# The low part of each dense weight tile: an accumulating DMA in place of a subtraction on VectorE

## The chip, the cores and the metric

The kernel runs on one core of one Trainium2 chip. The metric is the device time of one execution, in microseconds (us). Before the change the median of 3 runs is 2462.2 us (2461.52 to 2467.54).

## The reference

Two layers of a diffusion backbone on 512 latent tokens and 256 context tokens, 768 in all, with 1024 features. In each layer an adaLN-modulated RMSNorm feeds three token mixers (windowed attention, a bidirectional HGRN2 recurrence and a gated MLP over chunks) from one input projection; each branch is projected, gated and summed, and an output projection and a SwiGLU FFN follow, both with gated residuals. Context tokens are dropped from layer 1's queries onward, so that most of layer 1 works on 512 tokens.

```python
def merge(a, b, c, gate, w_br, w_o):
    g = jax.nn.sigmoid(gate.reshape(gate.shape[:-1] + (N_BRANCH, D_MODEL)))
    m = g[..., 0, :] * (a @ w_br[0]) + g[..., 1, :] * (b @ w_br[1]) + g[..., 2, :] * (c @ w_br[2])
    return m @ w_o

def swiglu(h, w_gate, w_up, w_down):
    return (jax.nn.silu(h @ w_gate) * (h @ w_up)) @ w_down
...
        y, yc = hybrid_mixer(h, hc, w_in[l], ...)
        x = x + g1 * y
        h = rmsnorm(x, norm2_g[l]) * (1.0 + sc2) + sh2
        x = x + g2 * swiglu(h, w_ffn_gate[l], w_ffn_up[l], w_ffn_down[l])
```

Everything is float32.

## The kernel before

Activations lie with the feature on the partition and the token along the row. Every large product goes through `dense`: it makes 128 output features for a range of tokens, from one weight tile of 128 input rows x `kt` groups (the k-rows) x 128 columns. TensorE multiplies in float32r, which keeps fewer bits than float32. So the weights and the activations are each split in a high part (the value rounded to float32r) and a low part (the rest), and each product is the sum of three: high x high, high weight x low activation, low weight x high activation. In `mms` these come in this order for each k-row, each in pieces of at most 512 columns. A tile with 8 k-rows is thus 24 products, each of 512, 768 (512 + 256) or 256 columns, and the first that needs the low weights is the third.

`load_w` makes a weight tile's parts. SyncE's queue loads `wr` from DRAM (`load_raw`, 3 buffers, shared with the tiles `wra` of the adaLN weights). ACT writes the high part `wh` by a copy (line 286, 2 buffers); VectorE writes the low part `wl` = `wr` - `wh` (line 287, 2 buffers). `load_w` is called 364 times, once for each dense product. Since `wh` and `wl` have two buffers, a tile's parts can be written once the product two before it is done with its buffers, that is, while the product just before it runs.

The products that the prediction speaks of, by stage, in each of the two layers:

- w_in: 34 tiles of 8 k-rows (heads of HGRN, keys, values, queries, the MLP's projections), among which the chains of HGRN and attention are woven in (`step_chain`).
- gate and branch: 24 pairs. The gate tile has 8 k-rows (from `w_in`), the branch tile 4 (from `w_branch`). ACT takes the tanh of the gate's result (line 1126), VectorE multiplies, and POOL adds to `macc` (line 1138).
- w_out: 8 tiles of 8 k-rows for each of two token blocks: 512 and 256 columns in layer 0, 256 and 256 in layer 1.
- FFN: 22 pairs of a gate and an up tile of 8 k-rows, with a silu of the gate's result between (line 1176), in four pieces (`FF_PIECES`, 5, 5, 6, 6). After each piece come 8 tiles of w_ffn_down with 5 or 6 k-rows; the last piece's are made for each of the two token blocks apart (512 and 256 columns, then 256 and 256).

Layer 0 has 768 tokens in all these; layer 1 has 512 from the queries on.

The order on each engine is set by the recording framework's scheduler, from the order in which the program is written and its own estimates of time; each engine, and each DMA queue, then runs its list in order. GpSimd's (POOL's) list holds tensor instructions, such as the sums of squares `sqa`, the rope products and the `macc` sums, and 16 DMAs that put the residual `X` into DRAM and bring it back (lines 588 and 594).

Of the kernel before, what the change touches and what calls it, by code (L numbers as in the profile page):

```python
# [9 lines left out]
F32 = mybir.dt.float32  # L10
# [6 lines left out]
P = 128  # L17
# [33 lines left out]
class Page:  # L51
    """A page of the static arena: one token row block ([P, T]) or two ([P, 2, T])."""
# [8 lines left out]
class Pages:  # L61
    """On-chip pages handed out in program order; the one that is free first by the estimate goes first."""
# [41 lines left out]
class Builder:  # L104
# [45 lines left out]
    def preload(self, func, after):  # L150
        """Has the activation table of func loaded as soon as after is there, before the data for it comes."""
        t = self.small("pre", 1)
        self.nc.scalar.activation(out=t, in_=after, func=func)

    # ---------------------------------------------------------------- setup
# [25 lines left out]
    def columns(self, name, items, queue):  # L181
        """Parameter vectors as columns of one tile, feature on the partition; yields between load and use."""
# [30 lines left out]
    def pcol(self, name, l=0, per=1):  # L213
        """Columns of a parameter: all of them, or those of layer l of per layers."""
        tile, r0, n = self.col[name]
        n //= per
        return self.par[tile][:, r0 + l * n:r0 + (l + 1) * n]
# [56 lines left out]
    # ------------------------------------------------------------- weights  # L274
# [5 lines left out]
    def load_w(self, wap, kt):  # L280
# [6 lines left out]
        nc.vector.tensor_tensor(out=o, in0=r, in1=h.bitcast(F32), op=ALU.subtract)  # L287
# [28 lines left out]
    def spent(self, us):  # L316
        """Advances the estimate of TensorE's clock and gives waiting chains their turns."""
# [20 lines left out]
    # --------------------------------------------------------------- adaLN  # L338
    def ada_fold(self, acc, part):
        """Partial products [128, 512] -> [128, 16]: sums over each 32 partitions, feature % 32 on the partition."""  # L340
# [6 lines left out]
    def ada_spread(self, l, units, parts, nb):  # L347
        """Sums the four partition groups of the parts of some units, each feature on its partition, and adds the bias."""
# [22 lines left out]
    def ada_units(self, l, units, nb):  # L371
        """Steps that make four feature tiles of the modulation for each unit while other work goes on."""
# [22 lines left out]
    def ada_first(self):  # L395
        """Scale and shift of the first norm, which everything waits for; yields within its work."""
# [23 lines left out]
    def ada_rows(self, u, w):  # L420
        """Four feature tiles of layer 0 on TensorE: two rows, turned into columns."""
# [31 lines left out]
    # --------------------------------------------------------------- norms  # L453
    def rstd(self, sq, chunks, inv_n):
        """1/sqrt(mean+eps) per token, a column for each chunk."""
# [15 lines left out]
    def spread(self, rs, chunks):  # L471
        """Spreads a column for each chunk over all partitions: one bank per 512 tokens."""
# [13 lines left out]
    def norm_sums(self, blk):  # L486
        """Squares of the residual's tokens of one block, summed over the feature tiles."""
# [12 lines left out]
    def settle(self, blk, apply, pace, spread=True):  # L500
        """A chain that norms one token block of the residual; apply takes the bank of rstd, by token % 512."""
# [22 lines left out]
    def norm_part(self, blk, rb, k0=0, k1=KD, pool=False):  # L524
        """h = rmsnorm(X)*(1+sc)+sh for one token block, split in float32r parts."""
# [37 lines left out]
    def split_pairs(self, srcs, t1, name):  # L563
        """srcs: float32 pairs, given back here -> act list of (hi, lo), pages held"""
# [14 lines left out]
    # ------------------------------------------------------------ residual  # L579
# [4 lines left out]
    def x_out(self, t1):  # L584
        """The residual isn't used inside a mixer: it waits in DRAM."""
# [41 lines left out]
    # ---------------------------------------------------------------- HGRN  # L627
# [152 lines left out]
    # ----------------------------------------------------------- attention  # L780
# [42 lines left out]
    def attn_queries(self, l, i, act, wcol, tq, ag):  # L823
        """Queries of two heads, each as a column stack of its high and low parts; their blocks join the chains."""
# [503 lines left out]
```

## Time and profile before

| | |
|---|---|
| median of 3 runs | 2462.2 us |
| the profiled execution's span | 2460.2 us |
| TensorE busy | 2410.8 us (98%) |
| VectorE busy | 1426.7 us (58%) |
| ScalarE (ACT) busy | 837.1 us (34%) |
| GpSimd (POOL) busy | 202.6 us (8%) |
| DMA engines, queue q1 (loads from DRAM) | 30.5% of 16 engines' span |
| mean granted TensorE clock | 0.998 |

The profiled execution took 2460.2 us from its first to its last instruction; the median of the runs stands 2.0 us over that. A row of the timeline gives the start in us from the span's start, the duration in us, the engine, the line, and what is written from what; in brackets stands how long the engine was idle before it and what ended that. A row of a group gives the count, the busy time in us, the mean duration in ns, and the idle time before. A row of waits gives the sum in us, the times, and the longest. A row of stretches gives the length and then the busy time and count of PE, PEld (TensorE's weight loads), DVE, ACT and POOL, the granted TensorE clock, the DMA share and GB/s. A row of DMA issues ends with the size in KB and the median us from issue to landing.

### The profile page before, as it was taken

Reading aid. Unit: us, or ns where it says so; the run is one execution under the profiler, and the core shown is the slowest. Engines: PE = TensorE matmul, PEld = TensorE weight load, DVE = VectorE, ACT = ScalarE, POOL = GpSimd, SP = SyncE. Lnnn points to the kernel's source line nnn. Section 1 sums busy time; section 2 is a strip of 40 time slices with the busy share of each in tenths; the row PEclk is TensorE's granted clock in tenths of the full one; section 3 lists DMA queues with packets and bytes.
Section 4 is the critical chain, followed back from the end, with each engine's and each line's share of the span. In section 5 each row is a group of like instructions: output and inputs, shape, how many; then the busy total and the mean of one; then the engine's idle time right before and its main releaser. Section 6 shows DMA issues by size and latency. Waiting matters only on the chain. (4 is left out here: it accounts for less than half of the span.)

```text
span 2460.2 us, 34161 instructions
## 1 busy us (share of the span) xinstructions
PE 2410.8 (98%) x13814; PEld 2074.5 (84%) x13814; DVE 1426.7 (58%) x2452; ACT 837.1 (34%) x1372; POOL 202.6 (8%) x143
## 2 busy tenths in 40 slices
PE   8999999999999999999999999999999999999998
PEld 3888888888888888888888888888888889888888
DVE  4688777875454374745353376668884337434335
ACT  3333344442222342221222253324453335322224
POOL 0000100000111210000000040101000122000001
PEclk9999999999999999999999999999999999999999
DMA  8222111123433243434344351112113335233334
GB/s 293 71 78 78 52 42 37 31 60 108 146 112 90 82 127 97 136 98 144 94 122 118 90 150 58 39 42 60 50 51 107 107 102 160 80 102 101 94 101 131
DMA packets 361869, 236.33 MB, mean 96 GB/s; under 512 B 8112, under 2 KB 333168, under 8 KB 361712
## 3 DMA queue, kind: packets, MB, share of 16 engines
q1 hardware_dynamic: 357776, 221.57, 30.5%
q0 software_dynamic: 2304, 10.49, 1.3%
q8 instruction: 109, 1.79, 0.3%
q10 hardware_dynamic: 1632, 2.10, 0.3%
q14 instruction: 48, 0.39, 0.0%
HBM read 226.78 MB, written 7.34 MB: 95 GB/s over the span
## 5 line engine op out<-in xcount | busy, mean ns | idle before, releaser
L286 ACT ACTIVATE wh<-wr 128x1024 fp32r<-128x1024 f32 (+2 forms) x364 | 344.7, 947 | 1042.7 <-PE pd L304 962.1
L287 DVE TENSOR_TENSOR wl<-wr,wh 128x1024 fp32r<-128x1024 f32 (+2 forms) x364 | 396.3, 1089 | 255.4 <-ACT wh L286 251.8
L304 PE MATMUL pd<-hh,wh 128*128 128x512 f32 (+1 forms) x1504 | 456.6, 359 | 1.0 <-DVE X L624 0.8
L304 PE MATMUL pd<-hh,wl 128*128 128x512 f32 (+1 forms) x1504 | 446.5, 353 | 0.3 <-DVE wl L287 0.3
L304 PE MATMUL pd<-hl,wh 128*128 128x512 f32 (+1 forms) x1504 | 443.9, 351 | 0.0
L304 PE MATMUL pd<-fl,wh 128*128 128x512 f32 (+1 forms) x1072 | 322.3, 352 | 0.0
L304 PE MATMUL pd<-fh,wl 128*128 128x512 f32 (+1 forms) x1072 | 321.8, 351 | 0.3 <-DVE wl L287 0.3
L304 PE MATMUL pd<-fh,wh 128*128 128x512 f32 (+1 forms) x1072 | 321.1, 351 | 0.6 <-ACT silu L1176 0.6
L304 PEld LDWEIGHTS pd<-hh,wl 128*128 128x128 f32 x1504 | 246.7, 188 | 37.6 <-DVE wl L287 0.8
L304 PEld LDWEIGHTS pd<-hl,wh 128*128 128x128 f32 x1504 | 246.5, 189 | 34.0
L304 PEld LDWEIGHTS pd<-hh,wh 128*128 128x128 f32 x1504 | 247.4, 189 | 31.3 <-ACT wh L286 1.2
L368 DVE SCALAR_TENSOR_TENSOR acc<-wra,sc,acc 128x512 f32<-128x512 f32 x224 | 162.1, 755 | 190.5 <-DMA wra<-in_w_ada 140.8
L304 PEld LDWEIGHTS pd<-fh,wl 128*128 128x128 f32 x1072 | 177.6, 188 | 30.0 <-DVE wl L287 1.2
L304 PEld LDWEIGHTS pd<-fh,wh 128*128 128x128 f32 x1072 | 176.9, 188 | 29.3 <-ACT silu L1176 0.8
L304 PEld LDWEIGHTS pd<-fl,wh 128*128 128x128 f32 x1072 | 177.4, 188 | 28.0
L304 PE MATMUL pd<-guh,wl 128*128 128x512 f32 (+1 forms) x576 | 174.8, 340 | 1.1 <-DVE wl L287 1.1
L304 PE MATMUL pd<-guh,wh 128*128 128x512 f32 (+1 forms) x576 | 175.0, 340 | 0.0
L304 PE MATMUL pd<-gul,wh 128*128 128x512 f32 (+1 forms) x576 | 174.5, 339 | 0.0
L1178 DVE TENSOR_TENSOR silu<-pd,silu 128x768 f32<-128x768 f32 (+1 forms) x44 | 36.2, 824 | 164.8 <-PE pd L304 164.8
L624 DVE SCALAR_TENSOR_TENSOR X<-pd,mod,X 128x256 f32<-128x256 f32 (+1 forms) x128 | 65.9, 546 | 94.7 <-PE pd L304 94.6
L304 PEld LDWEIGHTS pd<-guh,wl 128*128 128x128 f32 x576 | 99.5, 189 | 14.2 <-DVE wl L287 1.8
L304 PEld LDWEIGHTS pd<-gul,wh 128*128 128x128 f32 x576 | 99.5, 189 | 12.5
(224 smaller groups left out, 3362.0 us busy)
## 6 DMA issues: line engine op xcount, KB each, us to landing
wr<-in_w_in SPq DMA_DIRECT2D x116, 512.0 KB, 3.8
wra<-in_w_ada SPq DMA_DIRECT2D x80, 512.0 KB, 3.7
wr<-in_w_ffn_gate SPq DMA_DIRECT2D x44, 512.0 KB, 3.8
wr<-in_w_ffn_up SPq DMA_DIRECT2D x44, 512.0 KB, 3.9
wr<-in_w_ffn_down SPq DMA_DIRECT2D x48, 384.0 KB, 3.4
wr<-in_w_out SPq DMA_DIRECT2D x32, 512.0 KB, 4.1
wr<-in_w_branch SPq DMA_DIRECT2D x48, 256.0 KB, 2.8
wr<-in_w_ffn_down SPq DMA_DIRECT2D x32, 320.0 KB, 3.1
```

The source lines that it names most:

```text
L286: nc.scalar.activation(out=h, in_=r, func=AF.Copy)
L287: nc.vector.tensor_tensor(out=o, in0=r, in1=h.bitcast(F32), op=ALU.subtract)
L304: nc.tensor.matmul(ps[:, b0:b1], lhsT=w[:, k, :], rhs=x[:, b0:b1], start=b not in first, stop=(k == kt - 1 and i == 2), skip_group_check=True)
L368: nc.vector.scalar_tensor_tensor(out=acc[:, 0:512], in0=w, scalar=sc, in1=acc[:, 0:512], op0=ALU.mult, op1=ALU.add)
L624: self.nc.vector.scalar_tensor_tensor(out=self.X[m][:, c0:c1], in0=ps[:, c0:c1], scalar=gcol(b, m), in1=self.X[m][:, c0:c1], op0=ALU.mult, ...
L1178: nc.vector.tensor_tensor(out=s[:, 0:tt], in0=pu[:, 0:tt], in1=s[:, 0:tt], op=ALU.mult)
```

## The change

In `load_w` the subtraction on VectorE is gone. ACT, after the high copy, writes the negated raw tile into `wl`, rounded to float32r like the high part, so that `wl` holds minus the high part. Then GpSimd issues a DMA from `wr` to `wl`, both in SBUF, with `accum_op=ALU.add`: the DMA adds `wr` to what stands in `wl`, which leaves the low part. The DMA is issued once ACT's second copy is done, and the products with the low weights wait for its landing. `wr` is held until then too.

```diff
@@ -284,7 +284,8 @@
         lo = self.wl.tile([P, KD, P], F32R, tag="wl", name=self.nm("wl"))
         r, h, o = (t.rearrange("p k c -> p (k c)")[:, 0:kt * P] for t in (raw, hi, lo))
         nc.scalar.activation(out=h, in_=r, func=AF.Copy)
-        nc.vector.tensor_tensor(out=o, in0=r, in1=h.bitcast(F32), op=ALU.subtract)
+        nc.scalar.activation(out=o, in_=r, func=AF.Copy, scale=-1.0)
+        nc.gpsimd.dma_start(out=o, in_=r, accum_op=ALU.add)
         return hi, lo
```

The rest of the diff takes out docstrings and comments. Lines after 287 stand one further on in the changed kernel.

The scheduler orders the lists anew. Three places from the last gate and branch pairs of layer 1 show how. A name's first number is the tile's, the same in both kernels; 2762 and 2763 are the high and low part of one gate tile, 2767 and 2768 those of the branch tile after it, 2764 is that gate's result, 2769 the branch's, and the marks in brackets name the engines or queues (DMAHW: SyncE's loads, DMASW: POOL's DMAs) that the instruction waits for.

ACT's list, before:

```order
L286 ACTIVATE wh_2762_17409<-wr_2761_17407 128x1024 [waits DMAHW2_49,DVE_49,PE_49]
L1126 ACTIVATE gt_2756_17384<-pd_2755_17359 128x512 [waits PE_49]
L286 ACTIVATE wh_2767_17442<-wr_2766_17440 128x512 [waits DMAHW3_49,DVE_49,PE_49]
L576 ACTIVATE mh_2783_17527<-macc_2594_16457 128x512 [waits Pool_49]
L286 ACTIVATE wh_2771_17463<-wr_2770_17461 128x1024 [waits DMAHW4_49,DVE_49,PE_49]
```

and in the changed kernel:

```order
L286 ACTIVATE wh_2762_17669<-wr_2761_17667 128x1024 [waits DMAHW2_49,PE_49,Activation_49]
L1127 ACTIVATE gt_2756_17643<-pd_2755_17618 128x512 [waits PE_49]
L287 ACTIVATE wl_2763_17670<-wr_2761_17667 128x1024 [waits DMASW2_49]
L286 ACTIVATE wh_2767_17703<-wr_2766_17701 128x512 [waits DMAHW3_49,PE_49,Activation_49]
L287 ACTIVATE wl_2768_17704<-wr_2766_17701 128x512 [waits DMASW3_49,PE_49]
```

The negated copy of a gate tile stands behind the tanh of the gate before it; that of a branch tile follows its high copy directly.

POOL's list there, before:

```order
L1138 TENSOR_TENSOR macc_2567_16319<-macc_2567_16319,gt_2729_17222 128x512 [waits DVE_49,Pool_49]
L1138 TENSOR_TENSOR macc_2567_16319<-macc_2567_16319,gt_2738_17276 128x512 [waits DVE_49,Pool_49]
L1138 TENSOR_TENSOR macc_2594_16457<-macc_2594_16457,gt_2747_17330 128x512 [waits DVE_49,Pool_49]
L1138 TENSOR_TENSOR macc_2594_16457<-macc_2594_16457,gt_2756_17384 128x512 [waits DVE_49,Pool_49]
L1138 TENSOR_TENSOR macc_2613_16564<-macc_2613_16564,gt_2765_17438 128x512 [waits DVE_49,Pool_49]
```

and in the changed kernel:

```order
L1139 TENSOR_TENSOR macc_2594_16683<-macc_2594_16683,gt_2747_17587 128x512 [waits DVE_49,Pool_49]
L288 DMA wl_2759_17648<-wr_2757_17645 128x512 [waits DMAHW1_49,DMASW1_49,Activation_49]
L288 DMA wl_2763_17670<-wr_2761_17667 128x1024 [waits DMASW2_49,DMAHW2_49,PE_49,Activation_49]
L1139 TENSOR_TENSOR macc_2594_16683<-macc_2594_16683,gt_2756_17643 128x512 [waits DVE_49,Pool_49]
L288 DMA wl_2768_17704<-wr_2766_17701 128x512 [waits DMAHW3_49,DMASW3_49,Activation_49]
```

Each pair's sum stands between the DMA of the next gate tile and that of the next branch tile.

TensorE's list there, before:

```order
L304 MATMUL pd_2764_17413<-hh_1808_12377,wh_2762_17409 128x512 [waits Activation_49]
L304 MATMUL pd_2764_17413<-hl_1809_12378,wh_2762_17409 128x512
L304 MATMUL pd_2764_17413<-hh_1808_12377,wl_2763_17410 128x512 [waits DVE_49]
L304 MATMUL pd_2764_17413<-hh_1808_12377,wh_2762_17409 128x512
L304 MATMUL pd_2764_17413<-hl_1809_12378,wh_2762_17409 128x512
```

and in the changed kernel:

```order
L305 MATMUL pd_2764_17674<-hh_1808_12554,wh_2762_17669 128x512 [waits Activation_49]
L305 MATMUL pd_2764_17674<-hl_1809_12555,wh_2762_17669 128x512
L305 MATMUL pd_2769_17708<-brh_2703_17319,wh_2767_17703 128x512 [waits DVE_49,Activation_49]
L305 MATMUL pd_2769_17708<-brl_2704_17320,wh_2767_17703 128x512
L305 MATMUL pd_2764_17674<-hh_1808_12554,wl_2763_17670 128x512 [waits DMASW4_49]
L305 MATMUL pd_2764_17674<-hh_1808_12554,wh_2762_17669 128x512
```

The first two products of the branch tile now stand ahead of the gate tile's first product with low weights, which waits for the DMA.

## The prediction

> **What bounds the kernel now.** First the page: its span, the engines' shares, and the two groups of instructions that the change touches.
>
> ```profile
> span 2460.2 us, 34161 instructions
> PE 2410.8 (98%) x13814; PEld 2074.5 (84%) x13814; DVE 1426.7 (58%) x2452; ACT 837.1 (34%) x1372; POOL 202.6 (8%) x143
> L286 ACT ACTIVATE wh<-wr 128x1024 fp32r<-128x1024 f32 (+2 forms) x364 | 344.7, 947 | 1042.7 <-PE pd L304 962.1
> L287 DVE TENSOR_TENSOR wl<-wr,wh 128x1024 fp32r<-128x1024 f32 (+2 forms) x364 | 396.3, 1089 | 255.4 <-ACT wh L286 251.8
> ```
>
> TensorE is the bound: it idles 2460.2 - 2410.8 = 49.4 us in all. ACT's copies start when TensorE gives a buffer back (962.1 us of waiting for it), not when data arrives. So the question is how soon a low part is ready after that moment. Next the waits of TensorE on the low part:
>
> ```profile
> PE pd L304 <- DVE wl L287: 3.1, 7, 0.9
> PEld pd L304 <- DVE wl L287: 6.3, 12, 1.1
> ```
>
> Under 10 us: more than that the removed subtraction cannot give back. Then the timeline where the margin is smallest, a gate tile of layer 1 made while a branch tile is multiplied:
>
> ```profile
> 2006.58 0.39 PE L304 MATMUL pd<-hh,wl 128*128 128x512 f32 x1
> 2006.78 1.06 ACT L286 ACTIVATE wh<-wr 128x1024 fp32r<-128x1024 f32 x1 [2.04 <-PE pd L304]
> 2006.81 0.39 PE L304 MATMUL pd<-brh,wh 128*128 128x512 f32 x1
> 2007.75 0.58 ACT L1126 ACTIVATE gt<-pd 128x512 f32<-128x512 f32 x1
> 2007.87 1.23 DVE L287 TENSOR_TENSOR wl<-wr,wh 128x1024 fp32r<-128x1024 f32 x1 [2.40 <-ACT wh L286]
> 2009.53 0.39 PE L304 MATMUL pd<-hh,wh 128*128 128x512 f32 x1
> 2009.75 0.39 PE L304 MATMUL pd<-hl,wh 128*128 128x512 f32 x1
> 2009.98 0.39 PE L304 MATMUL pd<-hh,wl 128*128 128x512 f32 x1
> ```
>
> The old gate tile ends (2006.58), ACT copies the new one's high part at once, VectorE has the low part at 2009.10, and TensorE wants it at 2009.98: 0.9 us of slack. With two buffers, that race is run for every tile, and its length is the time of the dense product between.
>
> **The change part by part.** Removed: 364 subtractions on VectorE, off the path but for the waits above. Added on ACT: 364 copies with scale -1, priced as L286's. Added on POOL: 364 DMAs that read `wr` and add it to `wl`. Their time from issue to landing, L, is on no row: no DMA of the kernel accumulates. The nearest are POOL's DMAs of X and the 512 KB loads:
>
> ```profile
> q0 software_dynamic: 2304, 10.49, 1.3%
> xd<-X POOLq DMA_DIRECT2D x4, 512.0 KB, 4.1
> X<-xd POOLq DMA_DIRECT2D x4, 512.0 KB, 5.0
> wr<-in_w_in SPq DMA_DIRECT2D x116, 512.0 KB, 3.8
> DMA to landing us min/median/max: 3.5/5.5/13.1
> ```
>
> A plain 512 KB transfer of POOL's takes 4.1 or 5.0 us, 4.55 on average. Its packets took 1.3% of 16 engines' 2460.2 us, 512 us over 2304, so 222 ns for 4.55 KB, or 200 ns for a 4 KB row; 128 rows on 16 engines make 1.6 us. An accumulating row is read twice, once in `wr` and once in `wl`, so I add 1.6 us: L = 6.1 us for 8 k-rows. Splitting it into 2.9 fixed and 3.2 that scales gives 5.3 for 6 k-rows and 4.9 for 5. From below, the second read is free and SBUF is as quick as the fastest of those transfers: 3.5 us (1.9 + 1.6). From above, the whole 5.0 us is done twice: 10.0. I take 6.1, since one more pass over the data is the one addition that the operation forces.
>
> The Trainium skill (DMA: Bandwidth & Descriptors, Anatomy of one DMA) fits such a DMA as 2.0 us plus its bytes at 436 GB/s, an estimate of 3.2 us for 512 KiB; the rows above read 4.1 to 5.0 for the same bytes. By the page's figure the stalls worked out below would be about 110 us and the time some 2575 us.
>
> The chain for a new low part, from the moment the old tile's high buffer is free: high copy, (in some stages a tanh or silu of the old tile's result that stands between), negated copy, about 0.1 us to POOL, L.
>
> ```profile
> L286 ACT ACTIVATE wh<-wr 128x768 fp32r<-128x768 f32 x48 | 40.6, 845 | 119.8 <-PE pd L304 116.1 <-issue 1.2 <-ACT ot L1233 1.1
> L286 ACT ACTIVATE wh<-wr 128x640 fp32r<-128x640 f32 x32 | 23.7, 741 | 111.8 <-PE pd L304 111.8
> L1126 ACT ACTIVATE gt<-pd x48: 576/696/816, 532.5 to 2032.2; 128x768 f32<-128x768 f32 x24, 128x512 f32<-128x512 f32 x24
> L1176 ACT ACTIVATE silu<-pd x44: 576/686/797, 917.8 to 2408.9; 128x768 f32<-128x768 f32 x22, 128x512 f32<-128x512 f32 x22
> 2052.51 0.28 PE L304 MATMUL pd<-mh,wl 128*128 128x256 f32 x1
> 2052.63 0.28 PE L304 MATMUL pd<-mh,wh 128*128 128x256 f32 x1
> 1004.57 0.74 ACT L286 ACTIVATE wh<-wr 128x640 fp32r<-128x640 f32 x1 [4.46 <-PE pd L304]
> 1009.77 0.74 ACT L286 ACTIVATE wh<-wr 128x640 fp32r<-128x640 f32 x1 [4.46 <-PE pd L304]
> ```
>
> Back-to-back ACT instructions overlap by 0.1 us (1.06 then a start 0.97 later, above), so the ACT part with the 0.1 is 2.6 us with a 512-token tanh or silu between, 2.8 with a 768-token one, 2.1 with none, 1.7 for 6 k-rows and 1.5 for 5. TensorE steps 0.227 us per 512-column product (2009.53 to 2009.98 in two steps), 0.12 per 256 columns, and 768-token tiles of 5 k-rows come every 5.20 us, 0.347 for each of 15 products. The low part is due after the dense product between plus two products of the tile itself; in the gate stages two products of the next branch tile now stand ahead too. What is left for L is the room, and each pair of tiles stalls for L minus the room (the second tile of a pair gains what the first lost, so one stall per pair):
>
> - gate and branch, layer 1: 12 x 0.227 + 4 x 0.227 - 2.6 = 1.0 of room; 5.1 us for each of some 20 pairs (the first four hold attention work between): 102 us.
> - the same, layer 0: 16 x 0.347 - 2.8 = 2.7; 3.4 us x 22 = 75.
> - gate and up of the FFN, layer 1: 26 x 0.227 - 2.6 = 3.3; 2.8 x 22 = 62. Layer 0: 26 x 0.347 - 2.8 = 6.2, no stall.
> - w_out in 256-column blocks: 26 x 0.12 - 2.1 = 1.0; 5.1 x 12 pairs = 61. In 512: 3.8; 2.3 x 4 = 9.
> - w_ffn_down, 512 columns: 5 k-rows 2.4, 2.5 x 8 = 20; 6 k-rows 2.8, 2.5 x 8 = 20; 256 columns 0.7, 4.6 x 12 = 55; 768 tokens, 5 k-rows 4.4, 0.5 x 8 = 4; 6 k-rows none.
>
> Together 408 us. The w_in products of both layers are covered: two stretches of 390 and 395 us hold 34 tiles each, 11.5 us a tile against a chain of 8.2.
>
> ```profile
> 100.00:490.00 390.00, 381.41 (x2530) 342.34 (x2529) 310.89 (x631) 154.26 (x299) 27.59 (x16) 1.00 0.18 53
> 1435.00:1830.00 395.00, 382.70 (x2336) 330.70 (x2334) 295.84 (x561) 172.12 (x321) 44.78 (x30) 1.00 0.21 60
> POOL rs L468 <- DVE ms L465: 262.7, 16, 53.0
> POOL qf L787 <- DVE sh L785: 221.1, 7, 53.1
> ```
>
> But there POOL's tensor instructions wait for VectorE for tens of us, and DMAs now queue behind them in the program's order. Without that cover a tile costs up to its whole chain. I allow 25 us for 68 tiles.
>
> **The clock** adds to the stalls. Before, TensorE waited once for about 3 us:
>
> ```profile
> 76.89 0.66 PE L981 MATMUL wsps<-ident,wst 128*128 128x128 f32 x4 [3.08 <-DMA wst<-in_mlp_ws]
> 73.50:76.90 3.40, 0.32 (x4) 0.11 (x2) 0.00 (x0) 0.42 (x1) 0.00 (x0) 1.00 0.42 128
> 76.90:81.00 4.10, 4.10 (x22) 4.10 (x23) 0.06 (x1) 0.58 (x1) 0.00 (x0) 0.58 0.08 23
> ```
>
> After it the granted clock was 0.58 for 4.1 us, a loss of 4.1 x 0.42 = 1.7 us. Of the pairs above, 20 + 22 + 12 + 12 = 66 stall for over 3.3 us; if every one lost 1.7 it would be 112 us. One event doesn't tell how surely it follows, so I take half, 56. The Trainium skill (TensorE: Matmul & The Clock Gate, HAM oscillation) states that the window is about 3.4 us and free-running, so a pause a little longer is not sure to fill one; the pause here, 3.1 us by the wait, was enough.
>
> **Sum:** 2460.2 + 408 + 25 + 56 = 2949 us of span; the execution's span stands 2.0 us under the median of the runs, 2462.2, so **2950 us**.
>
> **The rivals.**
>
> *The accumulate costs no more than a plain copy*, L about 3.5. Stalls: 20 x 2.5 + 22 x 0.8 + 22 x 0.2 + 12 x 2.5 + 16 x 0.4 + 12 x 2.4 = 137 us, none over 3.3 us, so 2600 us. For it: DMAs within SBUF meet no DRAM. Against: `wl` has to be read as well.
>
> *Two passes, or slower*, L = 10: with 9.2 and 8.8 us for 6 and 5 k-rows (twice 3.4 + 1.2 and 3.4 + 1.0) the eleven kinds of pair above stall for some 960 us, nearly all of them over 3.3 us, with another 100 to 200 us of clock: about 3550 us. For it: one of the present DMAs took 13.1 us beside loads, and in the w_out stage of 256 columns a load and an accumulate of 512 KB would both be wanted every 5.4 us, half of 2 x 24 x 0.12 + 5.1. Against: on average the engines are far from full.
>
> *POOL's order decides*: each of the some 36 rs, Q, Y and rope instructions of the w_in stages holds the accumulate behind it for 3 us more, since the wait for VectorE now ends in a wait of TensorE. Price 36 x 3 = 108 us, 3060 us. Against: with 396 us less to do, VectorE answers sooner.
>
> *Not slower.* The low part lands within 1.0 us, inside every room above, or the DMA is not made as written; then only the waits on `wl` go, and the time is 2462 - 9 = 2453 us. It decides the other way from L = 1.0 up, where the first stage stalls; the quickest POOL transfer took 3.5, so the profile speaks plainly against it.
>
> **How the numbers follow.** Forecast (L between 4.8 and 8) 0.57; plain copy 0.13; two passes 0.17; POOL's order 0.10; not slower 0.03. The range runs from just above the plain-copy case to just under the two-pass case, 2610 to 3480 us, and leaves out about 2 in 10. A difference of 0.3%, 7 us, is what a measurement of this kernel tells from none. Slower 0.97, within 0.3% 0.015, faster 0.015.
>
> **What would show it.** Right: TensorE's idle time rises to over 400 us with the DMA wl<-wr as its largest releaser; queue q0 carries some 46,000 packets more (364 x 128 rows); that DMA takes about 6 us to landing for 512 KB; each gate and branch pair of layer 1 without attention work takes some 5 us more than its 36 x 0.227 = 8.2 us, and the gate and up tiles of layer 0 keep their length; the clock falls under 1.00 in the 256-column stages; VectorE's busy time falls by about 396 us and ACT's rises by about 345. Wrong: TensorE over 95% busy, a landing under 3.5 or over 10 us, or stalls in the w_in stages that end on POOL's own instructions.

## The result, and the profile after

The changed kernel takes 2971.7 us (median of 4 runs, 2960.87 to 2978.75), beside 2464.9 us of the kernel before (4 runs): a ratio of 1.203 (95% interval 1.200 to 1.206). It is slower by a fifth, and the forecast of 2950 us stands 0.7% under the result. The two large terms of its sum were both off, though, in opposite directions, so that so close a total is luck. The profiled execution is one of 2960.87 us, with a span of 2959.1.

First the page of the changed kernel: span, engines, POOL's DMA queue and the two groups that take the subtraction's place; then, from the view of DMA issues, the new DMA by size.

```profile
span 2959.1 us, 34878 instructions
PE 2591.0 (88%) x13814; PEld 2165.3 (73%) x13814; DVE 1064.9 (36%) x2088; ACT 1126.5 (38%) x1736; POOL 482.6 (16%) x507
q0 software_dynamic: 54720, 176.19, 32.3%
L287 ACT ACTIVATE wl<-wr 128x1024 fp32r<-128x1024 f32 (+2 forms) x364 | 340.4, 935 | 0.0
L288 POOL DMA_DIRECT2D wl<-wr x364 | 319.3, 877 | 2148.9 <-ACT wl L287 1863.2
```

```profile
wl<-wr POOLq DMA_DIRECT2D x236, 512.0 KB, 4.7
wl<-wr POOLq DMA_DIRECT2D x48, 384.0 KB, 4.6
wl<-wr POOLq DMA_DIRECT2D x48, 256.0 KB, 4.3
wl<-wr POOLq DMA_DIRECT2D x32, 320.0 KB, 4.4
```

TensorE is idle for 2959.1 - 2591.0 = 368.1 us, 318.7 more than before, and busy for 180.2 us more with the same 13814 products. The two add up to the 498.9 us that the span grew by. Most of the added busy time is a slower clock, but not all of it: the granted clock, 0.951 in the mean instead of 0.998, loses 0.049 x 2959.1 = 145 us against 0.002 x 2460.2 = 5 before, 140 more. The other 40 us are no slow clock. A product counts as busy for 0.39 us while the next one starts 0.227 us after it, and before a wait no next one covers the 0.16 us at its end; TensorE waits 229 times more often than before, which by this estimate makes 37 us. The landing takes 4.7 us for 512 KB, not 6.1, and depends little on the size: half the bytes save 0.4 us. VectorE got 362 us back, which bought nothing.

The waits that TensorE and SyncE's queue have in the changed kernel:

```profile
PE pd L305 <- DMA wl<-wr: 272.4, 160, 7.0
PE pd L305 <- ACT wh L286: 22.9, 28, 1.4
PE pd L305 <- DVE gt L1136: 15.6, 30, 0.8
PE pd L305 <- DVE macc L1133: 6.8, 11, 1.7
SPq L277 <- DMA wl<-wr: 2036.1, 295, 21.8
```

The landing is TensorE's largest releaser, as forecast. By stage it made TensorE wait for 6.7 and 8.1 us in w_in of the two layers, 43.3 and 75.1 in gate and branch, 13.3 and 18.2 in w_out, 29.7 and 78.0 in the FFN. The two rows that end on VectorE belong to the gate and branch stages but for 0.7 us, and these stages had no such wait before: the first two products of a branch tile, which now stand ahead, wait until VectorE has read an older result (lines 1133 and 1136). In the last row 295 loads of the next `wr` wait until an accumulation has landed; before, 270 waited for VectorE's subtraction, 1317.7 us in all.

The timeline of one gate and branch pair of layer 1 shows how it goes; it answers to the gate tile of the prediction.

```profile
2298.56 1.06 ACT L286 ACTIVATE wh<-wr 128x1024 fp32r<-128x1024 f32 x1 [8.55 <-PE pd L305]
2299.53 0.58 ACT L1127 ACTIVATE gt<-pd 128x512 f32<-128x512 f32 x1
2300.00 1.05 ACT L287 ACTIVATE wl<-wr 128x1024 fp32r<-128x1024 f32 x1
2301.36 0.86 POOL L288 DMA_DIRECT2D wl<-wr  x1 [11.17 <-ACT wl L287]
2302.22 0.39 PE L305 MATMUL pd<-brl,wh 128*128 128x512 f32 x1
2305.96 0.50 PE L305 MATMUL pd<-hh,wl 128*128 128x512 f32 x1 [3.35 <-DMA wl<-wr]
2307.06 0.63 PE L305 MATMUL pd<-hh,wl 128*128 128x512 f32 x1
2309.94 0.39 PE L305 MATMUL pd<-hh,wh 128*128 128x512 f32 x1
```

ACT needs 2.8 us from the old tile's end to POOL's issue, the DMA lands 4.6 us later, and TensorE has been waiting for 3.35 us. Then its products take 0.63 us instead of 0.39 for a while. The granted clock of the same place (length, then busy time of PE, PEld, DVE, ACT and POOL, the clock, DMA share, GB/s):

```profile
2302.60:2305.96 3.36, 0.01 (x1) 0.00 (x1) 0.69 (x1) 0.63 (x1) 1.74 (x2) 1.00 0.98 182
2305.96:2309.50 3.54, 3.54 (x9) 2.83 (x10) 0.00 (x0) 0.00 (x0) 0.00 (x0) 0.56 0.74 169
```

For 3.54 us after the pause the clock is 0.56. By stage, each from the first product with its activations to that of the next stage, the gate and branch stage of layer 1 and the FFN of layer 1 read so, before the change and then after it:

```profile
1827.90:2034.00 206.10, 206.03 (x959) 170.82 (x958) 89.89 (x147) 73.74 (x128) 27.63 (x19) 1.00 0.34 100
2083.40:2460.20 376.80, 368.71 (x1824) 312.47 (x1822) 159.21 (x234) 116.25 (x169) 12.86 (x13) 1.00 0.35 103
```

```profile
2018.10:2359.00 340.90, 254.78 (x959) 195.09 (x958) 47.56 (x100) 106.02 (x175) 61.44 (x65) 0.87 0.50 114
2452.50:2959.10 506.60, 408.66 (x1824) 323.89 (x1822) 76.56 (x150) 182.17 (x252) 82.10 (x97) 0.96 0.67 151
```

All eight stages, worked out from such rows (idle is the length less PE's busy time; us; in the changed kernel w_out of layer 0 holds 23 products fewer and w_in of layer 1 13 more, which moves a few us between neighbours):

| stage | length before | after | idle added | PE busy added | stall forecast |
|---|---|---|---|---|---|
| w_in, layer 0 | 482.6 | 489.6 | 5.9 | 1.2 | 25 with layer 1's |
| gate and branch 0 | 298.4 | 394.6 | 54.9 | 41.3 | 75 |
| w_out 0 | 73.0 | 94.7 | 14.9 | 6.8 | 29 |
| FFN 0 | 560.0 | 616.4 | 35.2 | 21.2 | 32 |
| w_in, layer 1 | 365.4 | 374.3 | 6.0 | 2.9 | (above) |
| gate and branch 1 | 206.1 | 340.9 | 86.0 | 48.8 | 102 |
| w_out 1 | 49.4 | 93.5 | 26.0 | 18.1 | 41 |
| FFN 1 | 376.8 | 506.6 | 89.8 | 40.0 | 129 |

### The profile page after: what moved, and what is told of

Same layout as the page of the kernel before. It is cut to its first block, busy times and chain, and to the rows that moved or that the text cites. A ratio compares the mean times of both kernels' runs of the same rounds, so it can differ in the third digit from the quotient of the medians.

```text
span 2959.1 us, 34878 instructions
## 1 busy us (share of the span) xinstructions
PE 2591.0 (88%) x13814; PEld 2165.3 (73%) x13814; DVE 1064.9 (36%) x2088; ACT 1126.5 (38%) x1736; POOL 482.6 (16%) x507
## 3 DMA queue, kind: packets, MB, share of 16 engines
q0 software_dynamic: 54720, 176.19, 32.3%
## 4 chain that ended last, share of the span: by engine, by line
PE 50%; DMA 24%; issue 17%; DVE 3%; ACT 3%; POOL 1%; SPq 0%; POOLq 0%; ACTq 0%; DVEq 0%
PE pd L305 43%; DMA wl<-wr 20%; DMA wra<-in_w_ada 2%; PE hl L690 2%; ACT wl L287 2%; PE pT L950 1%; PE ho L755 1%; POOL wl L288 1%; PE sc L895 1%; ACT wh L286 1%; PE pv L941 1%; DMA wr<-in_w_in 1%; PE hu L726 0%; PE pv L940 0%; DVE acc L369 0%
## 5 line engine op out<-in xcount | busy, mean ns | idle before, releaser
L288 POOL DMA_DIRECT2D wl<-wr x364 | 319.3, 877 | 2148.9 <-ACT wl L287 1863.2
L305 PE MATMUL pd<-hh,wl 128*128 128x512 f32 (+1 forms) x1504 | 478.8, 376 | 131.8 <-DMA wl<-wr 131.7
L305 PE MATMUL pd<-hh,wh 128*128 128x512 f32 (+1 forms) x1504 | 483.7, 379 | 3.0 <-ACT K L644 1.8
L305 PE MATMUL pd<-hl,wh 128*128 128x512 f32 (+1 forms) x1504 | 470.3, 369 | 0.0
L305 PEld LDWEIGHTS pd<-hh,wl 128*128 128x128 f32 x1504 | 263.8, 202 | 193.1 <-DMA wl<-wr 152.7
L287 ACT ACTIVATE wl<-wr 128x1024 fp32r<-128x1024 f32 (+2 forms) x364 | 340.4, 935 | 0.0
L305 PEld LDWEIGHTS pd<-hl,wh 128*128 128x128 f32 x1504 | 264.2, 201 | 40.2
L305 PEld LDWEIGHTS pd<-hh,wh 128*128 128x128 f32 x1504 | 265.1, 202 | 37.3 <-ACT K L644 1.9
L305 PE MATMUL pd<-guh,wl 128*128 128x512 f32 (+1 forms) x576 | 189.0, 366 | 68.6 <-DMA wl<-wr 68.3
L305 PE MATMUL pd<-guh,wh 128*128 128x512 f32 (+1 forms) x576 | 184.6, 357 | 11.7 <-ACT wh L286 8.4
```

Of the source, the lines that this page charges most:

```text
L287: nc.scalar.activation(out=o, in_=r, func=AF.Copy, scale=-1.0)
L288: nc.gpsimd.dma_start(out=o, in_=r, accum_op=ALU.add)
L305: nc.tensor.matmul(ps[:, b0:b1], lhsT=w[:, k, :], rhs=x[:, b0:b1], start=b not in first, stop=(k == kt - 1 and i == 2), skip_group_check=True)
```

## The experiments

Times are of single executions, but for the run with the subtraction put back in part, which has an interval. Stage lengths compare with the table. A stage that an edit leaves as it is in the changed kernel still differs from run to run, gate and branch of layer 0 between 382.7 and 394.6 us and the FFN of layer 0 between 616.4 and 626.2, so a difference of some 10 us in one stage says little.

**A plain copy in place of the accumulation.** This measures what the accumulation itself costs.

```diff
-        nc.gpsimd.dma_start(out=o, in_=r, accum_op=ALU.add)
+        nc.gpsimd.dma_start(out=o, in_=r)
```

> The low part is made by a plain copy of wr inside SBUF from the same place on POOL's queue: the addition of the negated high part is left out, so the low tile holds wr itself and the products use it as it is; everything else of the changed kernel stays. Theory (the length of one transfer from issue to landing, 4.7 us median for 512 KB, sets the pause): accumulating packets of 4096 bytes take 352 ns in the mean and plain ones 164, so the landing should come 1 to 2 us earlier, 2.7 to 3.7 us; about 118 pairs stall, each gets 1.0 to 2.0 us of TensorE's pause back and part of the slow clock behind it: 2961 - 118 x 1.4 - 40 = about 2755 us, between 2650 and 2850. Rival (the order on POOL, or holding the buffers, and not the transfer's own length): within 30 us of 2961.

Measured: 2717.2 us. POOL's queue and its DMAs on the page, and the landing of the new one:

```profile
q0 software_dynamic: 54720, 176.19, 19.1%
L288 POOL DMA_DIRECT2D wl<-wr x364 | 198.2, 544 | 2029.8 <-ACT wl L287 1836.5
wl<-wr POOLq DMA_DIRECT2D x236, 512.0 KB, 2.9
```

With the same packets and bytes the queue takes 19.1% x 2715.4 = 519 us of the 16 engines instead of 32.3% x 2959.1 = 956; less the 32 us of the kernel's other transfers (1.3% of 2460.2), 487 against 924, 1.9 times as much. So an accumulating packet is about two plain ones, as the forecast had it, and the landing of 512 KB goes from 4.7 to 2.9 us. The time to landing starts when POOL begins to issue, so 0.33 of these 1.8 us are POOL's (544 ns instead of 877). The 1.8 us a transfer are worth 244 us of the whole: TensorE is idle for 206.5 us instead of 368.1 and busy for 2508.9 instead of 2591.0. The theory's landing and time hold; of pause each of its 118 pairs got back 1.4 us, as it said, but the busy time gave 82 us and not 40. The Trainium skill (DMA: Bandwidth & Descriptors, Anatomy of one DMA) gives an estimate of 3.2 us for these bytes by its fit, near the 2.9 of the plain copy; no term for the accumulation stands in that fit, which is 1.5 us short of the 4.7 measured.

**The negated copy on VectorE.** It shortens the chain ahead of the DMA and leaves the DMA alone.

```diff
-        nc.scalar.activation(out=o, in_=r, func=AF.Copy, scale=-1.0)
+        nc.vector.tensor_scalar(out=o, in0=r, scalar1=-1.0, scalar2=None, op0=ALU.mult)
```

> VectorE, not ScalarE, makes the negated copy, beside ScalarE's high copy instead of behind it. Theory (stall = chain from the freed buffer to the landing, less the room): the chain loses most of one ScalarE copy, 0.94 us, where VectorE is free, and gains where VectorE is queued with other work; over about 118 stalled pairs 60 to 110 us: about 2870 us, between 2820 and 2930. Rival (POOL's queue or the DMA engines' throughput sets the pace): no change, 2961 within 20 us.

Measured: 2926.8 us, inside the theory's range, by way of gains and losses. The timeline of a pair like the one above with the end of the next one's pause, then four stretches of 3.41 us (the two that hold these pauses, and what follows each), and that of the whole gate and branch stage of layer 1:

```profile
2099.23 1.06 ACT L286 ACTIVATE wh<-wr 128x1024 fp32r<-128x1024 f32 x1 [11.97 <-PE pd L305]
2099.40 0.69 DVE L287 TENSOR_SCALAR wl<-wr 128x1024 fp32r<-128x1024 f32 x1 [11.46 <-PE pd L305]
2100.40 0.84 POOL L288 DMA_DIRECT2D wl<-wr  x1 [11.05 <-DVE wl L287]
2104.92 0.50 PE L305 MATMUL pd<-hh,wl 128*128 128x512 f32 x1 [1.64 <-DMA wl<-wr]
2115.81 0.50 PE L305 MATMUL pd<-hh,wl 128*128 128x512 f32 x1 [1.69 <-DMA wl<-wr]
```

```profile
2102.63:2106.04 3.41, 1.77 (x7) 1.16 (x8) 0.14 (x1) 0.00 (x0) 0.86 (x1) 1.00 0.95 169
2106.04:2109.45 3.41, 3.41 (x17) 2.81 (x16) 0.00 (x0) 0.00 (x0) 0.00 (x0) 1.00 0.70 199
2112.87:2116.28 3.41, 1.23 (x5) 0.72 (x5) 0.74 (x2) 0.09 (x1) 0.85 (x1) 1.00 0.96 177
2116.28:2119.69 3.41, 3.41 (x10) 2.63 (x9) 0.00 (x0) 0.00 (x0) 0.00 (x0) 0.50 0.66 158
2042.60:2326.80 284.20, 233.04 (x959) 179.08 (x958) 71.03 (x147) 73.93 (x128) 63.32 (x66) 0.94 0.61 137
```

POOL issues 1.17 us after ACT's copy began instead of 2.80, 1.63 sooner, and TensorE's pause is 1.64 us instead of 3.35, 1.71 shorter: what the chain loses the pause loses. The clock behind it is another matter: after a pause of 1.64 us it stays at 1.00, and after the next pair's, of 1.69 us, it is 0.50 for 3.41 us; 0.49 us of idle time stand 0.7 us ahead of both. What differs is where they fall. In the trace's records of the granted clock every slow stretch after the first 90 us starts a whole number of 3.41 us after the one before it, in this run as in all others, and what counts is how long TensorE was busy within the 3.41 us before such a mark: 1.77 us in the first pair, 1.23 in the second. Laid out so for the changed kernel, of the stretches at full clock all 57 with TensorE busy for under 45% are followed by a slow one, none of the 623 with over 70%, and 12 of the 77 between. So shorter pauses bring the slow clock in some pairs only; over the stage PE's busy time is 27.0 us above that of the kernel before, where the changed kernel has 48.8. The stage falls to 284.2 us, the one of layer 0 from 394.6 to 366.4. Where VectorE has other work the copy waits behind it: w_in of layer 0 grows from 489.6 to 507.2, the FFN of layer 0 from 616.4 to 650.5. There the copy begins up to 14.1 and 7.3 us after the high copy has begun, where ACT's began at most 5.5 and 1.7 us after it.

**Products with zeros while TensorE would wait.** This takes the pause away, not the chain.

```diff
+                for _ in range(fill if k == 0 and i == 2 else 0):
+                    b, b0, b1 = part[0]
+                    nc.tensor.matmul(ps[:, b0:b1], lhsT=self.zero, rhs=al[:, b0:b1], start=False, stop=False,
+                                     skip_group_check=True)
...
-                pg = self.dense(wcol(OFF_GT + idx * D + m * P), act, [(0, tt)])
+                pg = self.dense(wcol(OFF_GT + idx * D + m * P), act, [(0, tt)], fill=14 if l == 1 else 0)
```

Five kinds of small tiles have one buffer instead of four here, which makes space for the zeros.

> 14 products with a weight tile of zeros stand ahead of the first product with low weights in each gate tile of layer 1, so TensorE is busy while it would wait; the output isn't changed by them. Theory (the granted clock of 0.56 to 0.6 that follows each pause is caused by the pause): the products behind it run at 0.23 us instead of 0.42 us for some 3.5 us, about 1.9 us less per tile in about 24 tiles, the gate and branch stage of layer 1 goes from 340.9 to about 295 us and the whole to about 2915 us. Rival (the low clock comes from something else, or the pause alone makes the stage long): the stage stays within 10 us of 341 and its clock near 0.87.

Measured: 2948.7 us. The timeline of a pair, and the stage's stretch:

```profile
2100.05 0.85 POOL L292 DMA_DIRECT2D wl<-wr  x1 [15.35 <-PE pd L313]
2100.19 3.43 PE L310 MATMUL pd<-hl,zero 128*128 128x512 f32 x14
2104.62 0.50 PE L313 MATMUL pd<-hh,wl 128*128 128x512 f32 x1 [1.00 <-DMA wl<-wr]
```

```profile
2029.60:2340.10 310.50, 288.73 (x1282) 230.89 (x1281) 47.75 (x100) 108.58 (x176) 61.19 (x65) 0.99 0.55 125
```

The landing comes as late as ever (4.57 us after the issue), but the products behind it run at full speed, the stage's clock is 0.99 instead of 0.87, and the stage is 30.4 us shorter with 323 products more in it. So the pause causes the slow clock. The 46 us expected were too many: what the fillers did not cover (1.00 us here) is still waited for, and the two products of the branch tile no longer stand ahead. The whole gains only 12 us on the 2960.9 of the profiled changed kernel, not the 46 expected, since stages that this edit leaves alone are longer in this run (the FFNs by 9.8 and 6.6 us).

**The change's work in the shadow.** The kernel before, and in both feed-forward stages also the negated copy and the accumulating DMA, into an arena page that nothing reads.

```diff
         nc.vector.tensor_tensor(out=o, in0=r, in1=h.bitcast(F32), op=ALU.subtract)
+        if self.ffn:
+            pg = self.pair("sh")
+            sh = pg.ap.rearrange("p a b -> p (a b)")[:, 0:kt * P]
+            nc.scalar.activation(out=sh, in_=r, func=AF.Copy, scale=-1.0)
+            nc.gpsimd.dma_start(out=sh, in_=r, accum_op=ALU.add)
+            self.free(pg)
```

> The kernel before, with VectorE's subtraction, and in the feed-forward stages of both layers also the whole of the change's work in the shadow: ScalarE's negated copy of wr into an arena page and the accumulating DMA onto it, which nothing reads. What is left out of the change is only that TensorE waits for it. Theory (layer 1: TensorE's wait for the landing; layer 0: wr held until the landing makes loads late): the feed-forward of layer 1 stays near 377 us, that of layer 0 grows from 560 by 10 to 35 us, the whole comes to 2475 to 2505 us. Rival (the traffic of the DMA or ScalarE's and POOL's work slows the stages by itself): the feed-forward of layer 1 also grows by 60 us or more, and the whole is above 2560 us.

Measured: 2537.6 us, between the two. The FFN of layer 1 in this run, and its DMAs there (size, median us from issue to landing):

```profile
2125.00:2535.80 410.80, 383.12 (x1824) 319.55 (x1822) 161.53 (x234) 185.41 (x251) 82.19 (x95) 0.97 0.83 184
```

```profile
sh<-wr POOLq DMA_DIRECT2D x42, 512.0 KB, 6.0
wr<-in_w_ffn_up SPq DMA_DIRECT2D x21, 512.0 KB, 4.7
wr<-in_w_ffn_gate SPq DMA_DIRECT2D x20, 512.0 KB, 4.9
```

Though TensorE waits for none of it, the FFN of layer 1 grows by 34.0 us and that of layer 0 by 31.6 (591.6). The theory gave layer 0 its growth and was wrong on layer 1, where it had none; the rival had twice as much. The DMA engines are busy for 83% of layer 1's stage (73% of layer 0's), and the loads take 4.7 and 4.9 us to land where both took 3.8 before. VectorE's subtraction lasts as long there as before (median 1224 ns), but TensorE waits for its result for 10.0 us in 9 places, where the run with the copy alone, below, has 0.5. Three runs ask whether the copy, the held `wr` or the traffic does it.

*The copy alone.*

```diff
             nc.scalar.activation(out=sh, in_=r, func=AF.Copy, scale=-1.0)
-            nc.gpsimd.dma_start(out=sh, in_=r, accum_op=ALU.add)
```

> As the shadow run, but with ScalarE's negated copy alone; no accumulating DMA. Theories A and B: the copy is hidden, feed-forward stages of 560 to 566 and 377 to 382 us. Theory C (in the shadow run it was ScalarE's additional copy, queued ahead of the copies and the activation that TensorE's tiles wait for): 585 or more and 400 or more.

Measured: 565.4 and 383.4 us, +5.4 and +6.6 (2477.7 in all). So the copy is nearly hidden, and the DMA makes the other 26 to 27 us of each stage.

*The raw tiles on arena pages*, so that one held is no obstacle to the next load.

```diff
+        self.rawpg = self.pair("wr") if self.ffn else None
+        raw = (self.rawpg.ap.rearrange("p a b -> p (a b)")[:, 0:KD * P].rearrange("p (k c) -> p k c", c=P) if self.ffn else
+               self.wr.tile([P, KD, P], F32, tag="wr", name=self.nm("wr")))
```

> As the first shadow run (the kernel before, and in both feed-forward stages a negated copy of wr and the accumulating DMA of wr onto it, which nothing reads), but the raw tiles of these stages lie on arena pages instead of the three wr buffers, so that a raw tile held until the landing keeps no load back. Theory A (holding wr cost the 32 and 34 us): the feed-forward of layer 1 returns from 410.8 to 377 to 390 us, that of layer 0 from 591.6 to 560 to 575. Theory B (the transfer engines at 83%: loads and accumulations lengthen each other, and the loads come late whatever buffers there are): 400 us or more in layer 1, 585 or more in layer 0, with loads that take over 5 us from issue to landing.

Measured: 593.8 and 411.3 us, theory B's numbers. Loads of `up` took 6.4 us to land and those of `gate` 4.1. But the run is not clean: in the FFN of layer 1, 48 loads still waited for a landing (270 us in all), since pages come round too, and so it does not exclude that holding has a part.

*The DMA reads the high tile instead of `wr`.*

```diff
-            nc.gpsimd.dma_start(out=sh, in_=r, accum_op=ALU.add)
+            nc.gpsimd.dma_start(out=sh, in_=h.bitcast(F32), accum_op=ALU.add)
```

> As the shadow run (the kernel before, and in both feed-forward stages a negated copy and an accumulating DMA that nothing reads), but the DMA adds the high tile wh instead of wr: as many bytes and packets and as much work for ScalarE and POOL, but wr is free after the copies. Theory A (what cost the shadow run 32 and 34 us is that wr is held until the landing, so the next load is issued late): the feed-forward of layer 1 returns from 410.8 to 377 to 385 us, that of layer 0 from 591.6 to 560 to 570. Theory B (the transfer engines: with 83% of their time taken, loads and accumulations lengthen each other, whoever holds what): 400 us or more and 585 or more.

Measured: 632.2 and 434.9 us, worse than with `wr`, and 2598.0 in all. Above theory B's bounds, but not for its reason alone: `wh`, which has two buffers, is now held until the landing, and TensorE waits for ACT's high copy and the split behind it. No load waits for the landing here, and still those of 512 KB take 6.4 and 6.5 us. That loads and accumulations lengthen each other is thus seen in all three runs with the DMA; how the 26 to 27 us divide between that and held buffers stays open.

**More buffers for the change itself.** First the modulation's raw tiles `wra` alone, off the ring that they share with `wr`.

```diff
-            raw = self.wr.tile([P, 2, 512], F32, tag="wr", name=self.nm("wra"))
+            pg = self.pair("wra") if self.ffn else None
+            raw = (pg.ap.rearrange("p a b -> p (a b)")[:, 0:1024].rearrange("p (k c) -> p k c", c=512) if pg else
+                   self.wr.tile([P, 2, 512], F32, tag="wr", name=self.nm("wra")))
```

> The raw tiles of the modulation weights (wra), which share the ring of three wr buffers with the dense weights in the feed-forward of layer 0, lie on arena pages instead; the change stays. Theory (in that stage the loads are late since wr is held until the accumulating DMA has landed): the stage goes from 616.4 us back to 575 to 595 us, the whole to about 2930 us. Rival (that stage, too, waits for the landing of low weights alone): 616 within 8 us, and the whole 2960 within 15.

Measured: the FFN of layer 0 takes 627.0 us (616.4 before this edit), the whole 2971.3. The theory falls: sharing the ring is not what makes that stage longer. The rival has the whole right and the stage 3 us under what came.

Then the low tiles too, with the negated copy and the DMA ahead of the high copy.

```diff
+        lo = (self.lopg.ap.rearrange("p a b -> p (a b)")[:, 0:KD * P].rearrange("p (k c) -> p k c", c=P) if self.ffn else
+              self.wl.tile([P, KD, P], F32R, tag="wl", name=self.nm("wl")))
...
-        nc.scalar.activation(out=h, in_=r, func=AF.Copy)
         nc.scalar.activation(out=o, in_=r, func=AF.Copy, scale=-1.0)
         nc.gpsimd.dma_start(out=o, in_=r, accum_op=ALU.add)
+        nc.scalar.activation(out=h, in_=r, func=AF.Copy)
```

> In the feed-forward stages of both layers the low tiles (and the modulation's raw tiles) lie on arena pages, so that a low tile no longer waits for the end of the tile two before it, and the negated copy and its DMA are issued ahead of the high copy; elsewhere the change stays as it is. Theory (a race of latency for two buffers, with transfer engines and POOL far from full): the transfer runs well ahead, the feed-forward of layer 1 goes from 506.6 back to 377 to 400 us, that of layer 0 from 616.4 to 560 to 590 us, the whole to 2800 to 2850 us. Rival (throughput: POOL's issue, the DMA engines or the wr buffers limit how fast low tiles come): layer 1's stays above 450 us, and the whole above 2880 us.

Measured: 2955.7 us; the FFN of layer 0 takes 602.8 us, that of layer 1 518.4, no less than without. TensorE's waits in the FFN of layer 1, and a place in ACT's timeline:

```profile
PE pd L308 <- ACT silu L1187: 43.2, 19, 3.9
PE pd L308 <- DMA wl<-wr: 10.9, 10, 2.2
```

```profile
2604.97 0.74 ACT L289 ACTIVATE wl<-wr 128x640 fp32r<-128x640 f32 x1 [5.12 <-DMA wr<-in_w_ffn_down]
2606.57 0.57 ACT L1187 ACTIVATE silu<-pd 128x512 f32<-128x512 f32 x1
```

The number is the rival's, the reason is neither's. The wait for the low tile is gone (10.9 us), but a new one stands in its place: a negated copy for a later tile waits 5.12 us for its load at the head of ACT's list, and the silu that TensorE needs stands behind it.

Last, high copy first again, and `wr` on pages as well.

```diff
+        self.rawpg = self.pair("wr") if self.ffn else None
...
+        self.lopg = self.pair("wl", F32R) if self.ffn else None
...
+        if self.rawpg:
+            self.free(self.rawpg)
```

> The changed kernel with raw tiles, low tiles and the modulation's raw tiles of both feed-forward stages on arena pages, high copy first: neither two low buffers nor three raw buffers bind there. Theory (a low tile cannot be begun until ScalarE's queue gets to it, and ScalarE waits in order for one of two high buffers, so the chain of negated copy and transfer still begins only when a tile ends): PE still waits for the low tile, though less: feed-forward of layer 1 between 430 and 490 us, that of layer 0 between 575 and 605. Rival 1 (buffers alone): 377 to 400 us in layer 1. Rival 2 (transfer engines' throughput): above 490 us in layer 1, no less than in the changed kernel.

Measured: 2846.7 us. The FFN of layer 1, TensorE's waits in it, and the DMAs there:

```profile
2438.10:2844.90 406.80, 378.46 (x1824) 318.85 (x1822) 74.93 (x150) 183.18 (x251) 81.45 (x96) 0.97 0.86 185
```

```profile
PE pd L312 <- ACT wh L291: 14.3, 7, 5.1
PE pd L312 <- DMA wl<-wr: 3.2, 3, 1.6
```

```profile
wl<-wr POOLq DMA_DIRECT2D x43, 512.0 KB, 6.6
wr<-in_w_ffn_gate SPq DMA_DIRECT2D x19, 512.0 KB, 7.8
```

The stage falls from 506.6 to 406.8 us, 7 us above rival 1's band and far under the theory's: here the buffers, low and raw together, were the limit, and ACT's order hardly was. What is left, +30.0 us, is about what the shadow run has without a wait for the landing (+34.0), with the DMA engines at 86% and landings of 6.6 and 7.8 us. So of the 129.8 us that the change costs in the FFN of layer 1, about 100 are the wait for a landing with two low and three raw buffers, with its slow clock. The other 30 stay with more buffers too; that the transfers cost them is argued from the shadow run, not shown apart. In layer 0 the stage takes 610.3 us, 6 less than in the changed kernel and above the 605 of the theory: there the same edit helps little, and why is open.

**The DMA only where the forecast saw little cost.** w_in in both layers and gate and up in the FFN of layer 0; VectorE subtracts elsewhere.

```diff
+        if self.lodma:
+            nc.scalar.activation(out=o, in_=r, func=AF.Copy, scale=-1.0)
+            nc.gpsimd.dma_start(out=o, in_=r, accum_op=ALU.add)
+        else:
+            nc.vector.tensor_tensor(out=o, in0=r, in1=h.bitcast(F32), op=ALU.subtract)
```

> The DMA makes low parts only in the projections w_in of both layers and in gate and up of layer 0's feed-forward, where the forecast had stalls of 0 to 25 us; VectorE subtracts everywhere else as before. Theory (the cost sits in the stages with little room): w_in's +16 us stay, the feed-forward of layer 0 keeps part of its +56, the others return to their old lengths: 2465 + 16 + 10 to 40 = 2490 to 2520 us. Rival 1 (no cost where the room is longer than the landing, and VectorE's time saved is worth something): 2465 or less. Rival 2 (the cost is spread over the program): above 2560 us.

Measured: 2493.2 us (4 runs, 2491.78 to 2499.13), a ratio of 1.009 (95% interval 1.006 to 1.012) to the kernel before. w_in adds 11.9 and 7.7 us, the FFN of layer 0 13.9, and every other stage is back within 0.7 us of its old length. The theory holds: the cost sits where the room is short, and where it is long the VectorE time saved is worth nothing. None of the runs is faster than the kernel before.

## Why the prediction was right, and where its steps were not

**What bounds it, and the race of the two buffers: right.** The time went where the list of rooms said. Shorten the chain by 1.63 us and the pause shrinks by 1.71; take the buffers away as a limit and TensorE's wait for the low tile falls from 78.0 to 3.2 us in the FFN of layer 1.

**L, the time from issue to landing: mis-sized.** 6.1 us was taken, 4.7 measured. The second read, for which 1.6 us were added, is there: 1.8 us between the plain and the accumulating run, 0.33 of them POOL's longer issue. What failed is the base, 4.55 us, taken from POOL's transfers of the residual to and from DRAM; the plain copy inside SBUF lands in 2.9. The two bounds, 3.5 and 10.0, held. The split into 2.9 us fixed and 3.2 that scale with the bytes failed too: half the bytes save 0.4 us.

**The rooms: right within a tenth.** With the measured landings (4.7 us for 8 k-rows, 4.6 for 6, 4.4 for 5) the same list gives, in the order of the stages from gate and branch of layer 0 on, 44, 18, 23, 74, 30 and 85: 274 us. TensorE's waits for the landing in these stages were 43.3, 13.3, 29.7, 75.1, 18.2 and 78.0: 257.6. The idle time that was added there is longer, 306.8 us. In the gate and branch stages the other 22 us are the waits for VectorE, 21.7 us by the view of waits: the prediction counted the two early products of a branch tile as room and not that they need a buffer which VectorE has to read first. In the other stages part of it is the wait for ACT's high copy, 22.9 us in all.

**Half of the possible clock loss: wrong.** 56 us were allowed; by the granted clock it was about 140. The prediction halved a loss of 1.7 us because one event does not tell how surely it follows, and it counted only the 66 pairs that it saw stall for over 3.3 us, 112 us in full. The zeros show that the pause causes the loss. By the clock of the stage rows the gate and branch stages lost (1 - 0.92) x 394.6 + (1 - 0.87) x 340.9 = 76 us, 1.8 for each of the forecast's 42 pairs there: full price, not half. The FFNs, where the list has 12 pairs over 3.3 us (20 us in full), lost about (1 - 0.98) x 616.4 + (1 - 0.96) x 506.6 = 33 us, and in the gate and branch stage of layer 0 the idle time is 54.9 us over 22 pairs, 2.5 a pair, and the loss still 32: less than 3.3 us of pause is enough. Nor was there only one event before the change: a second pause, of 2.61 us, was followed by a clock of 0.69 in the stretch from 93 to 97 us.

```profile
94.32 1.37 PE L777 MATMUL tp<-ident,vf 128*128 128x128 f32 x6 [2.61 <-ACT vf L652]
```

```profile
93.00:97.00 4.00, 2.68 (x14) 2.68 (x15) 1.84 (x2) 2.86 (x5) 0.00 (x0) 0.69 0.22 47
```

The border was wrong in kind: as the run with the negated copy on VectorE shows, what decides is not the pause's length alone but the busy share of fixed stretches of 3.41 us.

The Trainium skill (TensorE: Matmul & The Clock Gate, HAM oscillation) has the rule that no idle gap should exceed some 3.4 us, which is what the prediction's border of 3.3 us amounts to. Here the measurement differs: an idle time of 0.49 and 1.69 us, with two products between, was enough. The Trainium skill (TensorE: Matmul & The Clock Gate, What's actually happening) has a window of 3413 ns that runs freely; the traces agree, with slow stretches that start whole multiples of 3.41 us apart.

**25 us for w_in: at most 15.9 measured** (7.0 and 8.9), by the lengths of the stages; the waits for the landing there are 14.8 us. In the shadow runs, which leave w_in as it was, layer 1's is 4 to 8 us longer as well, so that not all of its 8.9 need be the DMA's. POOL's own instructions ahead of the DMA cost no more than that, so the 108 us of the rival by POOL's order did not come.

**Missed: the traffic and the buffers held by it.** The prediction let the new DMAs cost nothing but their own landing. In the FFN stages, the shadow run shows, the DMA engines go to 73 and 83%, in layer 1 loads land 1 us later, and 26 to 27 us a stage are lost with nobody waiting for the DMA's result.

So the mechanism was right, and the closeness of the total is luck: 408 + 25 us of stalls came out as 319, and 56 us of clock as 180 of busy time, 140 of them clock; the errors of -114 and +124 us cancel. Of the signs that the prediction named, TensorE's idle time stayed under the 400 us (368.1), VectorE's busy time fell by 362 us and ACT's rose by 289 instead of 396 and 345, and POOL's queue carries 52,416 packets more, not 46,000, 16 more for each DMA. **The rivals:** a plain copy's cost would have been 2717 us, not 2600: the idle time grows by 157 us, near the 137 of that rival, but the busy time, to which it gave nothing, by 98. L = 10 and L under 1.0 are excluded by the landing.

## What to carry to other kernels

Replacing an instruction of a half-idle engine by a DMA trades about 1 us of work for 4 to 5 us of latency, and where two buffers are all there is, what counts is the time from a buffer's release to the landing, less the work between: work that out per stage before counting engine shares. If TensorE's waits then grow from fractions of a microsecond to two or three, price the slow clock behind each pause in full, some 1.7 us; waits that leave TensorE busy for over 70% of every 3.41 us go free. And look at the transfer engines' share in the busiest stage with the new bytes in it, an accumulating byte counted twice; with more buffers the wait goes, but the traffic stays.

## What the runs showed of the hardware

- An accumulating DMA inside SBUF takes the transfer engines 1.9 times as long as a plain one of the same bytes, and lands 512 KB in 4.7 us instead of 2.9; half as many bytes land only 0.4 us sooner.
- POOL spends 877 ns on issuing one, 319.3 us in all for 364, and 544 ns on a plain one.
- The clock goes by fixed stretches of 3.41 us: one in which TensorE is busy for under 45% is followed by one at half the clock (57 of 57 in the changed kernel), one over 70% by none (0 of 623), and in between it is open (12 of 77). So a pause of 1.69 us (1.23 us busy in its stretch) costs 1.7 us and one of 1.64 us (1.77 us busy) nothing; 14 products with zeros in the pause avert it.
- Loads and accumulations side by side lengthen each other: with 86% of the transfer engines' time taken, 512 KB loads landed in 6.3 and 7.8 us and accumulations in 6.6, against 3.8 for the loads before the change and 4.7 for the accumulations over the whole changed kernel.
